# A hybrid decoder trunk on one core: the low part of the attention result made on GpSimd, and forget-gate steps with one operand in PSUM

## The chip, the cores and the metric

The kernel runs on one NeuronCore of a Trainium2 chip. A core has five engines with instruction queues of their own: TensorE (PE in the profile; its weight loads are shown as PEld), VectorE (DVE), ScalarE (ACT), GpSimd (POOL) and SyncE (SP, which here issues most DMAs). Each engine runs its queue in order; between engines, semaphores keep the order. SBUF is the working memory, and PSUM the memory into which TensorE writes. The metric is the device time of one execution in microseconds.

## The reference

Two layers over 512 tokens of width 1024 in float32. The first has a short gated convolution and a pooling mixer, the second (the odd layer) a forgetting attention and a Conformer convolution; each is followed by an output projection, a layer norm, a SwiGLU with 2816 hidden channels, and a layer norm. The part that the change touches is the attention of the odd layer:

```
log_f = log_sigmoid(p[..., gate columns] + forget_b)          # 8 heads
cum   = cumsum(log_f, axis=1)
logits[t, s] = q_t . k_s / 8 + cum[t] - cum[s],  causal
y_c   = softmax(logits) @ v                                   # 8 heads of 64
y     = concat([y_c, y_d]) @ w_out                            # y_d: the Conformer branch
```

## The kernel before

**Numbers.** Every float32 operand of a large product is split in two: a high part, which ACT writes as a copy rounded to the format fp32r, and a low part, the source minus the high part. A product is three matmuls (`mm3`, lines 88 to 90: high by high, low by high, high by low). The helper `split` makes both parts; its line 84 is the copy on ACT and its line 85 the subtraction, on DVE unless another engine is passed. In the profile, line 85 is therefore most of the subtractions in the program, told apart by the tile that they write.

**Order of the work.** A scheduler orders the instructions of the engines from a simulated timeline, with priorities; in the attention the order on TensorE is that of the code (a manual schedule), and the other engines are still ordered by the scheduler. `wk`, `wtp` and `rawp` are pools of SBUF buffers (2, 8 and 3 buffers to a tag), so an instruction that writes a new tile waits until the tile that held the buffer has been read.

**The odd layer**, in the order of its stages:

- *Conformer input and convolution* (`conv`, lines 448 to 469). Four blocks of 128 channels and 31 taps. Two and a large part of a third run on DVE, one multiply-add of 128x512 to a tap with the running sum in PSUM (L466, tile `cv`, with `convs` for the last); ACT starts such a block at L454. The rest are products on ACT (L459, `prod`) that GpSimd adds up (L460, `convs`). L469 on DVE joins a DVE and a GpSimd part. These run in the background of all that follows.
- *Forget gates* (`forget_gates`): some twenty small steps on 128x32 values, mostly on DVE, in the SBUF tile `gates`: z, -|z|, its exponential e, r = 1/(2+e), s1 = e*r, s2 = s1*s1, a polynomial in s2 (L510, seven steps) and lf, split into `lfh` and `lfl`.
- *Sums* (`cumulate`): eight matmuls (L575) against a triangle into the PSUM bank `py`; the rows and their negatives, each in two parts, go to the tile `aug` (L578 and L580 on ACT, L579 and L581 on DVE). `add_cum` (L634) copies rows of it by DMA into the operand tiles `qk` of a head.
- *Projections*: queries and keys of a head (`qk_proj`, weights `wqh` and `wql`, the latter made by GpSimd for four heads' worth at a time), values (`value_proj`, matmuls of 128x256 in the bank `fl`). `operands` (L623 to L629) splits a head's query and key and thereby frees its `fl` bank; L624 and L627 are its DVE steps.
- *Attention*, a loop over heads h = 0 to 7. The table `SEQ` sets the order in each round: S0, S1, S2 are scores and softmax of head h (L651 to L662; L658 and L661 on DVE, L660 and L662 on ACT), T0 and T1 the transposes of the probabilities of head h-1 with their split into `th` (ACT) and `tl` (DVE), W the product with the values of head h-1 (`weigh`, L692 on TensorE), and F0 to F3 a part of the projection of head h+2 or, in the last two rounds, of the output projection. With the statistics of the convolution (`conv_stats`, L711 to L717, in rounds 4 and 5) goes a power on GpSimd (L166, `rs`); `conv_swish` (L731 to L740, in round 6) ends that branch.
- *`weigh`* adds the two halves of a head's result in `yatt` (L696, L697); after the second head of a pair it splits the pair into `yc`, the left operand of the output projection. There are four pairs, j = 0 to 3.
- *The late affine* (`late_affine`, L202) multiplies and adds the norm's parameters to the residual stream, 16 instructions on GpSimd in this layer.
- *Output projection*: its weights `w` are loaded by `load_split` with the low part on GpSimd (L85, 128x1024).

Of the kernel before, what the change touches and what calls it, by code (L numbers as in the profile page):

```python
# [14 lines left out]
ALU = mybir.AluOpType  # L15
# [11 lines left out]
NH = 8  # L27
# [31 lines left out]
def trunk(ctx, tc, x, ev_w_in, ev_conv_w, ev_pool_w, ev_pool_scale, ev_w_out, od_w_in,  # L59
# [13 lines left out]
    def psum(tag=None):  # L73
        tag = tag or next(turn)
        return banks.tile([P, 512], F32, tag=tag, name=tag, bufs=BANKS[tag])

    def tpsum():
        return psum("tp")
# [3 lines left out]
    def split(hi, lo, src, eng=None):  # L82

        nc.scalar.activation(hi, src, AF.Copy)  # L84
        (eng or nc.vector).tensor_tensor(lo, src, f32(hi), op=ALU.subtract)  # L85
# [344 lines left out]
    def odd_mixer():  # L430
# [3 lines left out]
        V = nc.vector  # L434
        G = nc.gpsimd
        with tc.tile_pool(name="odd", bufs=1) as op:
# [6 lines left out]
            yc = [op.tile([P, 2, 2, S], F32R, tag="yc", name="yc", bufs=2) for _ in range(2)]  # L443
# [31 lines left out]
            def forget_gates():  # L475

                fraw = rawp.tile([P, KD, P], F32, tag="raw", name="fraw")[:, :, :NH]
                nc.sync.dma_start(fraw, w_in[:, FC:FC + NH].rearrange("(k p) c -> p k c", p=P))
                fw = op.tile([P, KD, 2 * NH], F32R, tag="fw", name="fw")
                split(fw[:, :, 0:NH], fw[:, :, NH:], fraw)  # L480
                fb = small32[:, 32:64].rearrange("p (t h) -> p t h", h=NH)
                nc.sync.dma_start(fb, bass.AP(tensor=od_forget_b.tensor, offset=od_forget_b.offset,
                                              ap=[[0, P], [0, NT], [1, NH]]))
                pf = psum("py")
                for k in range(KD - 1):
                    nc.tensor.matmul(pf[:2 * NH, :], fw[:, k, :], xh[:, k, :], start=k == 0, stop=False)
                for k in range(KD):
                    nc.tensor.matmul(pf[:NH, :], fw[:, k, :NH], xl[:, k, :], start=False, stop=False)
                nc.tensor.matmul(pf[:2 * NH, :], fw[:, KD - 1, :], xh[:, KD - 1, :], start=False, stop=True)
                fT = wk.tile([2 * NH, S], F32, tag="sg", name="fT")  # L490
                nc.scalar.activation(fT, pf[:2 * NH, :], AF.Copy)
                tp = tpsum()
                for t in range(NT):
                    nc.tensor.transpose(tp[:, t * 16:(t + 1) * 16], fT[:, t * P:(t + 1) * P], ident[:16, :16])
                tpv = tp[:, :64].rearrange("p (t c) -> p t c", c=16)
                small = wk.tile([P, S], F32, tag="h", name="gates")
                z, nz, e, r, s1, s2, w, lf = (small[:, i * 32:(i + 1) * 32].rearrange("p (t h) -> p t h", h=NH)
                                              for i in range(8))
                V.tensor_tensor(z, tpv[:, :, 0:NH], fb, op=ALU.add)
                V.tensor_tensor(z, tpv[:, :, NH:], z, op=ALU.add)  # L500
                V.scalar_tensor_tensor(nz, z, -1.0, z, op0=ALU.mult, op1=ALU.min)
                nc.scalar.activation(e, nz, AF.Exp)

                V.tensor_scalar(r, e, 2.0, None, op0=ALU.add)
                V.reciprocal(r, r)
                V.tensor_tensor(s1, e, r, op=ALU.mult)
                V.tensor_tensor(s2, s1, s1, op=ALU.mult)
                V.tensor_scalar(w, s2, 1.0 / 17.0, None, op0=ALU.mult)
                for c in (15, 13, 11, 9, 7, 5, 3):
                    V.scalar_tensor_tensor(w, w, 1.0 / c, s2, op0=ALU.add, op1=ALU.mult)  # L510
                V.scalar_tensor_tensor(w, w, 1.0, s1, op0=ALU.add, op1=ALU.mult)
                V.tensor_scalar(z, z, 0.0, None, op0=ALU.min)
                V.scalar_tensor_tensor(lf, w, -2.0, z, op0=ALU.mult, op1=ALU.add)
                split(lfh, lfl, lf)

            for j in range(4):
                if j == 0:
                    ws = [load_cols(w_in, DC + i * DH + n * P, eng=G if n >= DG else None)
                          for n in range(DFIRST) for i in range(2)]
                    accs = [psum(tag) for _, tag in zip(ws, ("sc", "sc", "py", "fl"))]  # L520
                    project(accs, ws, SPLIT)
                elif j >= DFIRST:
                    ws = [load_cols(w_in, DC + i * DH + j * P, eng=G) for i in range(2)]
                    accs = [psum("fl" if j % 2 else "sc") for _ in range(2)]
                    project(accs, ws, ALL)
                pv, pg = accs[2 * j:2 * j + 2] if j < DFIRST else accs
                sg = wk.tile([P, S], F32, tag="sg", name="sg")
                nc.scalar.activation(sg, pg, AF.Sigmoid)
                hp = op.tile([P, S + KCONV - 1], F32, tag="hp", name="hp", bufs=4)
                nc.gpsimd.memset(hp[:, 0:KCONV - 1], 0.0)  # L530
                V.tensor_tensor(hp[:, KCONV - 1:], pv, sg, op=ALU.mult)
                with tc.high_priority(offset=-CP):
                    conv(hp, j)
                if j == FPOS:
                    forget_gates()
# [146 lines left out]
            y32 = {}  # L682

            def weigh(h, th, tl):
                j, i = h // 2, h % 2
                if i == 0:
                    y32[j] = wk.tile([P, S], F32, tag="h", name="yatt")
                py = psum("py")
                terms = [(p, kb) for kb in range(NT) for p in (th, tl)]
                terms.append(terms.pop(1))  # L690
                for m, (p, kb) in enumerate(terms):
                    nc.tensor.matmul(py[:, kb * P:], vs[kb][:, h, :, :].rearrange("p a c -> p (a c)"),  # L692
                                     p[:, OFF[kb]:OFF[kb] + S - kb * P],
                                     start=m == 0, stop=m == len(terms) - 1)
                tmp = wk.tile([HD, S], F32, tag="sg", name="tmp")
                nc.scalar.activation(tmp, py[up, :], AF.Copy)  # L696
                V.tensor_tensor(y32[j][i * HD:(i + 1) * HD, :], py[lo, :], tmp, op=ALU.add)  # L697
                if i == 1:
                    split(yc[j // 2][:, j % 2, 0, :], yc[j // 2][:, j % 2, 1, :], y32[j])

            yds = []

# [95 lines left out]
            for h in range(NH):  # L798
                probs, stages = softmax(h, T[h])
                for i, op_ in enumerate(seq):  # L800
                    g = h if i > seq.index("W") else h - 1
                    if op_[0] == "S":
                        stages[int(op_[1])]()
                    elif op_[0] == "F":
                        fill[h][int(op_[1])]()
                    elif g >= 0 and op_ == "W":
                        weigh(g, *pt[g][:2])
                    elif g >= 0 and op_[0] == "T":
                        if g not in pt:
                            pt[g] = transpose_p(last if g < h else probs)  # L810
                        pt[g][2 + int(op_[1])]()
                    run((h, i))
                last = probs
# [4 lines left out]
            for t, op_ in zip(B, (tail + [None, None])[:2]):  # L818
                proj.first(0, (t,))
                if op_:  # L820
                    pt[NH - 1][2 + int(op_[1])]()
            weigh(NH - 1, *pt[NH - 1][:2])
            for i in range(1, 3):
                proj.first(i, [t for t in range(NT) if t not in done[i]])
# [33 lines left out]
```

## Time and profile before

| | |
|---|---|
| median of 3 runs | 1119.0 us (1117.41 to 1124.48) |
| profiled execution, its own time | 1118.16 us |
| span in its profile, first to last instruction | 1116.4 us |
| mean granted clock of TensorE | 0.991 |
| attention of the odd layer, with its convolution | about 535 to 715 us of the span |

The page of the profile gives busy time by engine, then the span in 40 slices (a digit is a tenth of the slice; PEclk is the clock granted to TensorE), then the chain of work that ended last, and groups of instructions by line. Rows of single instructions show start, length, engine, line, operation, output and inputs (partitions x elements, type), and, in brackets, how long the engine had stood idle before it and for whom it waited.

### The profile page before, as it was taken

To read this page: it belongs to the slowest core of one execution; us is meant where nothing else is said; L and a number is where in the kernel's file an instruction comes from. 1 tells how busy PE (TensorE), PEld (TensorE's weight loads), DVE (VectorE), ACT (ScalarE), POOL (GpSimd) and SP (SyncE) were. 2 spreads that over 40 slices of the span, in tenths; PEclk is the share of its full clock that TensorE was granted. 3 is DMA by queue.
4 is the path that set the end of the run, shared out by engine and by line. 5 is a ranking of instruction groups with operands and counts; after the bars stand their busy time and mean duration, and the time that the engine had idled before them with its cause. 6 is when DMAs were issued, how large, how long until landed. Compare 5 with 4: busy or idle time off the path is not lost.

```text
span 1116.4 us, 13508 instructions
## 1 busy us (share of the span) xinstructions
PE 1079.8 (97%) x5371; PEld 910.6 (82%) x5371; DVE 547.4 (49%) x821; ACT 395.5 (35%) x613; POOL 176.1 (16%) x160
## 2 busy tenths in 40 slices
PE   7999999999999999999999958999999999999997
PEld 7888898888888888889878746889888888888886
DVE  4845364633333322436689978564553333332426
ACT  4333134222233221223566838634232222222210
POOL 2000300000000000012797942520000000000003
PEclk9999999999999999999999979999999999999999
DMA  6423403343333222440332221333343333332312
GB/s 202 125 88 116 144 1 114 114 116 101 102 97 94 95 95 95 135 130 2 87 104 75 88 85 58 95 95 95 95 132 95 95 95 100 104 98 95 109 42 76
DMA packets 150332, 108.30 MB, mean 97 GB/s; under 512 B 5256, under 2 KB 131768, under 8 KB 150270
## 3 DMA queue, kind: packets, MB, share of 16 engines
q1 hardware_dynamic: 149648, 107.11, 31.9%
q8 instruction: 42, 0.69, 0.2%
q10 hardware_dynamic: 622, 0.34, 0.1%
q14 instruction: 20, 0.16, 0.1%
HBM read 103.17 MB, written 2.10 MB: 94 GB/s over the span
## 4 chain that ended last, share of the span: by engine, by line
PE 85%; DVE 7%; ACT 3%; POOL 3%; issue 1%; DMA 1%; SPq 0%; POOLq 0%; ACTq 0%
PE fl L88 11%; PE fl L89 11%; PE fl L90 11%; PE sc L89 9%; PE sc L90 9%; PE sc L88 9%; PE py L88 4%; PE py L89 4%; PE py L90 4%; PE cv L89 4%; PE cv L90 4%; PE cv L88 4%; DVE cv L466 2%; POOL convs L460 1%; DVE yc L85 1%
## 5 line engine op out<-in xcount | busy, mean ns | idle before, releaser
L84 ACT ACTIVATE w<-raw 128x1024 fp32r<-128x1024 f32 x176 | 185.9, 1060 | 538.1 <-PE sc L89 180.7
L85 DVE TENSOR_TENSOR w<-raw,w 128x1024 fp32r<-128x1024 f32 x148 | 180.7, 1224 | 287.5 <-ACT w L84 287.5
L85 POOL TENSOR_TENSOR w<-raw,w 128x1024 fp32r<-128x1024 f32 x28 | 67.4, 2415 | 450.6 <-ACT w L84 427.5
L89 PE MATMUL sc<-xl,w 128*128 128x512 f32 (+1 forms) x360 | 129.9, 361 | 0.0
L90 PE MATMUL sc<-xh,w 128*128 128x512 f32 (+1 forms) x360 | 129.6, 361 | 0.0
L88 PE MATMUL sc<-xh,w 128*128 128x512 f32 (+1 forms) x360 | 129.4, 362 | 0.0
L88 PE MATMUL fl<-xh,w 128*128 128x512 f32 (+1 forms) x352 | 128.6, 366 | 0.0
L89 PE MATMUL fl<-xl,w 128*128 128x512 f32 (+1 forms) x352 | 128.4, 365 | 0.0
L90 PE MATMUL fl<-xh,w 128*128 128x512 f32 (+1 forms) x352 | 128.3, 365 | 0.0
L166 POOL TENSOR_TENSOR rs<-rs,neghalf 128x1 f32<-128x1 f32 x20 | 14.4, 722 | 417.9 <-DVE rs L165 417.9
L89 PEld LDWEIGHTS sc<-xl,w 128*128 128x128 f32 x360 | 68.0, 189 | 10.3
L90 PEld LDWEIGHTS sc<-xh,w 128*128 128x128 f32 x360 | 68.0, 189 | 10.2
L88 PEld LDWEIGHTS sc<-xh,w 128*128 128x128 f32 x360 | 67.6, 189 | 10.4
L89 PEld LDWEIGHTS fl<-xl,w 128*128 128x128 f32 x352 | 66.5, 189 | 10.6
L88 PEld LDWEIGHTS fl<-xh,w 128*128 128x128 f32 x352 | 66.4, 189 | 10.6
L90 PEld LDWEIGHTS fl<-xh,w 128*128 128x128 f32 x352 | 66.3, 189 | 10.6
L89 PE MATMUL fl<-w,hh 128*128 128x512 f32 (+1 forms) x176 | 66.3, 377 | 0.0
L88 PE MATMUL fl<-w,hh 128*128 128x512 f32 (+1 forms) x176 | 66.1, 376 | 0.0
L90 PE MATMUL fl<-w,hl 128*128 128x512 f32 (+1 forms) x176 | 66.1, 376 | 0.0
L466 DVE SCALAR_TENSOR_TENSOR cv<-hp,par,cv 128x512 f32<-128x512 f32 x84 | 62.9, 749 | 5.2 <-ACT cv L454 3.9
L89 PE MATMUL py<-xl,w 128*128 128x512 f32 (+1 forms) x160 | 58.9, 368 | 0.0
L88 PE MATMUL py<-xh,w 128*128 128x512 f32 (+1 forms) x160 | 58.9, 368 | 0.0
(360 smaller groups left out, 2066.9 us busy)
## 6 DMA issues: line engine op xcount, KB each, us to landing
raw<-in_ffn_w_in SPq DMA_DIRECT2D x88, 512.0 KB
raw<-in_ffn_w_out SPq DMA_DIRECT2D x44, 512.0 KB
raw<-in_od_w_in SPq DMA_DIRECT2D x20, 512.0 KB
raw<-in_ev_w_in SPq DMA_DIRECT2D x16, 512.0 KB
raw<-in_ev_w_out SPq DMA_DIRECT2D x8, 512.0 KB
raw<-in_od_w_out SPq DMA_DIRECT2D x8, 512.0 KB
x<-in_x SPq DMA_DIRECT2D x4, 512.0 KB
qk<-qk SPq DMA_DIRECT2D x16, 128.0 KB
```

The source lines that it names most:

```text
L84: nc.scalar.activation(hi, src, AF.Copy)
L85: (eng or nc.vector).tensor_tensor(lo, src, f32(hi), op=ALU.subtract)
L88: nc.tensor.matmul(acc, lh, rh, start=start, stop=False)
L89: nc.tensor.matmul(acc, lh, rl, start=False, stop=False)
L90: nc.tensor.matmul(acc, ll, rh, start=False, stop=stop)
L166: nc.gpsimd.tensor_tensor(rs[:, 1:2], rs[:, 0:1], neghalf, op=ALU.pow)
L460: G.tensor_tensor(acc, acc, prod[:, i % 2, :], op=ALU.add)
L466: V.scalar_tensor_tensor(acc if i == KCONV - 1 else part, hp[:, i:i + S], tap(i), part, op0=ALU.mult, op1=ALU.add)
```

## The change

`weigh` passes GpSimd to `split` for the first three head pairs, so that the low part of `yc` is made there and not on DVE; the last pair stays on DVE. The high part stays on ACT.

In `forget_gates`, most of the values move from the SBUF tile to a PSUM bank (tag `py`), and where a step reads two of them, one is read from PSUM and the other from SBUF. For that, three values (z, s1 and s2) are made twice, once in each memory: three more DVE steps, written as `zp`/`zs`, `s1p`/`s1` and `s2p`/`s2`.

```
-                small = wk.tile([P, S], F32, tag="h", name="gates")
-                z, nz, e, r, s1, s2, w, lf = (small[:, i * 32:(i + 1) * 32].rearrange("p (t h) -> p t h", h=NH)
-                                              for i in range(8))
+                view = lambda tile, i: tile[:, i * 32:(i + 1) * 32].rearrange("p (t h) -> p t h", h=NH)
+                bank = psum("py")
+                small = wk.tile([P, S], F32, tag="h", name="gates")
+                zp, nz, e, r, s1p, s2p, w, lf = (view(bank, i) for i in range(8))
+                z, zs, r_, s1, s2, zmin = (view(small, i) for i in range(6))
                 V.tensor_tensor(z, tpv[:, :, 0:NH], fb, op=ALU.add)
-                V.tensor_tensor(z, tpv[:, :, NH:], z, op=ALU.add)
-                V.scalar_tensor_tensor(nz, z, -1.0, z, op0=ALU.mult, op1=ALU.min)
+                V.tensor_tensor(zp, tpv[:, :, NH:], z, op=ALU.add)
+                V.tensor_tensor(zs, tpv[:, :, NH:], z, op=ALU.add)
+                V.scalar_tensor_tensor(nz, zp, -1.0, zs, op0=ALU.mult, op1=ALU.min)
                 nc.scalar.activation(e, nz, AF.Exp)
                 V.tensor_scalar(r, e, 2.0, None, op0=ALU.add)
-                V.reciprocal(r, r)
-                V.tensor_tensor(s1, e, r, op=ALU.mult)
-                V.tensor_tensor(s2, s1, s1, op=ALU.mult)
-                V.tensor_scalar(w, s2, 1.0 / 17.0, None, op0=ALU.mult)
+                V.reciprocal(r_, r)
+                V.tensor_tensor(s1p, e, r_, op=ALU.mult)
+                V.tensor_tensor(s1, e, r_, op=ALU.mult)
+                V.tensor_tensor(s2p, s1p, s1, op=ALU.mult)
+                V.tensor_tensor(s2, s1p, s1, op=ALU.mult)
+                V.tensor_scalar(w, s2p, 1.0 / 17.0, None, op0=ALU.mult)
                 for c in (15, 13, 11, 9, 7, 5, 3):
                     V.scalar_tensor_tensor(w, w, 1.0 / c, s2, op0=ALU.add, op1=ALU.mult)
                 V.scalar_tensor_tensor(w, w, 1.0, s1, op0=ALU.add, op1=ALU.mult)
-                V.tensor_scalar(z, z, 0.0, None, op0=ALU.min)
-                V.scalar_tensor_tensor(lf, w, -2.0, z, op0=ALU.mult, op1=ALU.add)
+                V.tensor_scalar(zmin, zp, 0.0, None, op0=ALU.min)
+                V.scalar_tensor_tensor(lf, w, -2.0, zmin, op0=ALU.mult, op1=ALU.add)
                 split(lfh, lfl, lf)
...
-                    split(yc[j // 2][:, j % 2, 0, :], yc[j // 2][:, j % 2, 1, :], y32[j])
+                    split(yc[j // 2][:, j % 2, 0, :], yc[j // 2][:, j % 2, 1, :], y32[j], G if j < 3 else V)
```

Since the scheduler orders the engines anew, instructions that the diff does not name change places on DVE, ACT, GpSimd and SP, and the eight matmuls of the sums on TensorE. The prediction shows where. In the changed kernel the lines behind the gates are numbered 5 higher (L579 is L584 there).

GpSimd's queue from the last convolution sums to the statistics, as the change moves it, with rows in the form line, operation, output and inputs, shape, count; `x_76` and `x_77` are tiles of the residual stream:

```order
-L202 TENSOR_TENSOR x_76<-x_76,gb 128x512
-L85 TENSOR_TENSOR wql<-raw,wqh 128x8x64
+L202 TENSOR_TENSOR x_76<-x_76,gb 128x512 x2
+L85 TENSOR_TENSOR wql<-raw,wqh 128x8x64 x2
 L202 TENSOR_TENSOR x_77<-x_77,gb 128x512 x2
-L460 TENSOR_TENSOR convs<-convs,prod 128x512
 L85 TENSOR_TENSOR wql<-raw,wqh 128x8x64 x2
-L85 TENSOR_TENSOR w<-raw,w 128x1024
-L460 TENSOR_TENSOR convs<-convs,prod 128x512
-L85 TENSOR_TENSOR w<-raw,w 128x1024
+L85 TENSOR_TENSOR yc<-yatt,yc 128x512
+L85 TENSOR_TENSOR w<-raw,w 128x1024 x2
```

Both convolution sums have left this place (they stand earlier in the queue), the weights of heads 6 and 7 come in pairs, and the subtraction for the first head pair stands behind the last of them.

DVE between the low part of the gates and head 0's softmax, before:

```order
L85 TENSOR_TENSOR lfl<-gates,lfh 128x32
L466 SCALAR_TENSOR_TENSOR cv<-hp,par,cv 128x512
L85 TENSOR_TENSOR v<-fl,v 128x4x64
L466 SCALAR_TENSOR_TENSOR cv<-hp,par,cv 128x512 x4
L579 TENSOR_TENSOR aug<-py,aug 8x512
```

and in the changed kernel:

```order
L85 TENSOR_TENSOR lfl<-py,lfh 128x32
L466 SCALAR_TENSOR_TENSOR cv<-hp,par,cv 128x512
L85 TENSOR_TENSOR v<-fl,v 128x4x64
L466 SCALAR_TENSOR_TENSOR cv<-hp,par,cv 128x512
L85 TENSOR_TENSOR v<-fl,v 128x4x64
L466 SCALAR_TENSOR_TENSOR cv<-hp,par,cv 128x512 x2
L466 SCALAR_TENSOR_TENSOR convs<-hp,par,cv 128x512
L584 TENSOR_TENSOR aug<-py,aug 8x512
```

Between the gates' low part and the first row of sums stand the same number of convolution steps, but the last of them now ends a block.

## The prediction

> **What bounds the kernel now.** I read the page first: TensorE is busy almost everywhere, so only a stage in which it is not can give time back.
>
> ```profile
> PE 1079.8 (97%) x5371; PEld 910.6 (82%) x5371; DVE 547.4 (49%) x821; ACT 395.5 (35%) x613; POOL 176.1 (16%) x160
> PE   7999999999999999999999958999999999999997
> DVE  4845364633333322436689978564553333332426
> POOL 2000300000000000012797942520000000000003
> PEclk9999999999999999999999979999999999999999
> ```
>
> The digit 5 of PE and the 7 of PEclk stand in slice 24 (642 to 670 us), in the attention of the odd layer, where DVE and POOL are also at their fullest. So next come busy times per engine in short windows there (length; then PE, PEld, DVE, ACT, POOL; clock), and the list of who waited for whom.
>
> ```profile
> 577.00:587.00 10.00, 7.17 (x57) 6.82 (x56) 9.87 (x14) 4.39 (x8) 9.87 (x8) 1.00 0.45 112
> 635.00:643.00 8.00, 7.41 (x41) 5.71 (x39) 7.91 (x9) 5.30 (x12) 8.00 (x7) 1.00 0.16 36
> 643.00:654.00 11.00, 0.28 (x2) 0.00 (x0) 10.94 (x8) 1.39 (x3) 7.34 (x6) 0.66 0.27 95
> 654.00:660.50 6.50, 6.46 (x21) 5.09 (x22) 4.06 (x12) 3.84 (x11) 0.00 (x0) 0.52 0.00 0
> ...
> PE py L692 <- DVE tl L85: 11.2, 2, 10.8
> ACT pr L662 <- DVE sm L661: 14.9, 7, 10.6
> ```
>
> For 11 us TensorE does nothing, and it then runs 6.5 us at a granted clock of 0.52. The instructions in order of time show why (start, length, engine, line):
>
> ```profile
> 638.13 1.30 POOL L202 TENSOR_TENSOR x<-x,gb 128x512 f32<-128x512 f32 x1
> 638.85 12.04 DVE L85 TENSOR_TENSOR yc<-yatt,yc 128x512 fp32r<-128x512 f32 x1
> 639.36 1.31 POOL L85 TENSOR_TENSOR wql<-raw,wqh 128x512 fp32r<-128x512 f32 x1
> 640.60 2.57 POOL L202 TENSOR_TENSOR x<-x,gb 128x512 f32<-128x512 f32 x2
> 643.08 1.30 POOL L460 TENSOR_TENSOR convs<-convs,prod 128x512 f32<-128x512 f32 x1
> 644.30 2.52 POOL L85 TENSOR_TENSOR wql<-raw,wqh 128x512 fp32r<-128x512 f32 x2
> 646.74 2.38 POOL L85 TENSOR_TENSOR w<-raw,w 128x1024 fp32r<-128x1024 f32 x1
> 649.04 1.30 POOL L460 TENSOR_TENSOR convs<-convs,prod 128x512 f32<-128x512 f32 x1
> 650.88 0.73 DVE L466 SCALAR_TENSOR_TENSOR cv<-hp,par,cv 128x512 f32<-128x512 f32 x1
> 654.04 0.69 PE L692 MATMUL py<-tl,v 128*128 128x384 f32 x1 [10.77 <-DVE tl L85]
> ...
> L85 DVE TENSOR_TENSOR yc<-yatt,yc x4: 678/801/12035, 638.9 to 713.8; 128x512 fp32r<-128x512 f32 x4
> ```
>
> One subtraction on DVE, the low part of the first head pair, takes 12.04 us where the shortest of its kind takes 0.68. It ends at 650.89, just after GpSimd's unbroken row of two-operand instructions ends (649.04 + 1.30 = 650.34). Both its inputs lie in SBUF; DVE's neighbours that read an operand from PSUM (L466, 0.73) are not stretched. So I read it as DVE waiting for a read path that GpSimd doesn't let go while its queue is full. DVE runs in order: behind it stand L661, the tl splits that TensorE needs (10.77) and ACT's softmax (10.6).
>
> The page "SBUF — State Buffer" of the Trainium skill (Who interferes with whom) says that a DVE instruction with two SBUF inputs and a GpSimd one that reads SBUF exclude each other, and that the later one blocks until the first finishes. The trace agrees on who meets, not on how long: by that rule this subtraction would have got in at 639.43 and little would be there to gain; eight more GpSimd instructions went first.
>
> The gates, in the same dense stretch, show it small (shortest/median/longest ns): 183 with an operand in PSUM, up to 1339 without.
>
> ```profile
> L499 DVE TENSOR_TENSOR gates<-tp,small x1: 183/183/183, 573.6 to 573.6; 128x32 f32<-128x32 f32 x1
> L512 DVE TENSOR_SCALAR gates<-gates x1: 1154/1154/1154, 577.6 to 577.6; 128x32 f32<-128x32 f32 x1
> L504 DVE TENSOR_SCALAR gates<-gates x1: 1339/1339/1339, 578.6 to 578.6; 128x32 f32<-128x32 f32 x1
> L506 DVE TENSOR_TENSOR gates<-gates x1: 1219/1219/1219, 581.4 to 581.4; 128x32 f32<-128x32 f32 x1
> ...
> 586.51 0.36 PE L88 MATMUL fl<-w,xh 128*128 128x256 f32 x1 [2.83 <-DVE qk L627]
> ```
>
> **The change, term by term**, against the profiled execution: 1118.16 us (span 1116.4 and 1.76 around it); the median of the three is 1119.0, 0.8 above.
>
> *1. The stall at 638.85 goes: -10.8.* GpSimd takes the subtraction, in another place of its queue:
>
> ```order
> -L460 TENSOR_TENSOR convs<-convs,prod 128x512
>  L85 TENSOR_TENSOR wql<-raw,wqh 128x8x64 x2
> -L85 TENSOR_TENSOR w<-raw,w 128x1024
> -L460 TENSOR_TENSOR convs<-convs,prod 128x512
> -L85 TENSOR_TENSOR w<-raw,w 128x1024
> +L85 TENSOR_TENSOR yc<-yatt,yc 128x512
> +L85 TENSOR_TENSOR w<-raw,w 128x1024 x2
>  L166 TENSOR_TENSOR rs<-rs,neghalf 128x1 x2
>  L85 TENSOR_TENSOR w<-raw,w 128x1024
> +L85 TENSOR_TENSOR yc<-yatt,yc 128x512
>  L166 TENSOR_TENSOR rs<-rs,neghalf 128x1 x2
> ```
>
> It stands behind the last wql and is needed only by the output projection. It costs GpSimd what a wql costs:
>
> ```profile
> L85 POOL TENSOR_TENSOR wql<-raw,wqh 128x512 fp32r<-128x512 f32 x16 | 20.5, 1300 | 5.5 <-ACT wqh L84 5.5
> ```
>
> So 3 x 1.3 = 3.9 us on an engine that then waits (0.00 busy from 654 to 660.5 above). The two convolution sums that stood last now run before the late affine, so the normalization's statistics needn't wait for them. With the DVE instruction gone, five DVE steps of 0.15 to 0.7 lie between 638.85 and tl, which is then ready near 642; TensorE began its wait at 643.27 (654.04 - 10.77), so the whole of it goes. Bounds: 8, if head 4 then waits for GpSimd's queue, dry at 650.3, and 10.8.
>
> *2. The slow clock goes: -2.5.* In 6.5 us at clock 0.52 TensorE loses at most 6.46 x 0.48 = 3.1; I take 2.5, since some of it would be waits for the softmax. Bounds 0 and 3.1.
>
> *3. The gates: +1.0.* DVE loses its stretched steps (0.97 + 1.16 + 1.04 = 3.2 over 0.18 each in the three rows above, beside smaller ones) and gets three more steps of 0.18. That takes away TensorE's 2.83 at 583.7. But DVE's order changes too. Before, from the low part of the gates to the rows of sums (aug) and on to head 0's softmax:
>
> ```order
> L85 TENSOR_TENSOR lfl<-gates,lfh 128x32
> L466 SCALAR_TENSOR_TENSOR cv<-hp,par,cv 128x512
> L85 TENSOR_TENSOR v<-fl,v 128x4x64
> L466 SCALAR_TENSOR_TENSOR cv<-hp,par,cv 128x512 x4
> L579 TENSOR_TENSOR aug<-py,aug 8x512
> L85 TENSOR_TENSOR v<-fl,v 128x4x64
> L466 SCALAR_TENSOR_TENSOR cv<-hp,par,cv 128x512
> L581 SCALAR_TENSOR_TENSOR aug<-py,aug 8x512
> ```
>
> and in the changed kernel (L579 is L584 there, L581 is L586):
>
> ```order
> L85 TENSOR_TENSOR v<-fl,v 128x4x64
> L466 SCALAR_TENSOR_TENSOR cv<-hp,par,cv 128x512 x2
> L466 SCALAR_TENSOR_TENSOR convs<-hp,par,cv 128x512
> L584 TENSOR_TENSOR aug<-py,aug 8x512
> L466 SCALAR_TENSOR_TENSOR cv<-hp,par,cv 128x512 x2
> L586 SCALAR_TENSOR_TENSOR aug<-py,aug 8x512
> L466 SCALAR_TENSOR_TENSOR cv<-hp,par,cv 128x512 x2
> ```
>
> A convolution block now ends ahead of L584, and the two cv steps behind it open the next block. In all five convolution steps come ahead of the first softmax that came behind it, 5 x 0.73 = 3.7 us at most, and on TensorE the eight matmuls of the sums stand 34 value matmuls later.
>
> ```profile
> 596.78 0.28 PE L89 MATMUL fl<-w,xh 128*128 128x256 f32 x1
> 596.89 0.56 PE L575 MATMUL py<-tri,lfh 128*8 128x512 f32 x2
> 600.86 0.68 DVE L579 TENSOR_TENSOR aug<-py,aug 8x512 fp32r<-8x512 f32 x1
> 602.69 0.68 DVE L581 SCALAR_TENSOR_TENSOR aug<-py,aug 8x512 fp32r<-8x512 f32 x1
> 605.03 0.50 PE L653 MATMUL sc<-qk 68*128 68x512 f32 x1
> ```
>
> From 586.51 to 596.78 stand 86 value matmuls, 0.12 each. Without the wait the row starts at 583.7; 120 of them now precede the sums: 583.7 + 14.4 = 598.1, not 596.9. From the sums' start to head 0's scores (L653) the copies, L579, L581 and their DMAs took 8.1 us; kept, the scores start at 606.2, 1.2 later than 605.03, and TensorE, which has only 24 value matmuls left behind the sums (598.1 + 8 x 0.28 + 24 x 0.12 = 603.2), waits 3 us there. I take +1.0. Bounds: -2.8, if the chain of copies shortens as much, and +3. The five steps moved forward leave DVE less behind 635, which is in term 1.
>
> *4. Given back in head 4: +1.1.* When everything comes some 12 us earlier, the second out-projection weight does not: its DMA waits until GpSimd's third of the last wqls frees the buffer, before at about 645.6 (644.30 + half of 2.52), and takes 3.6 us (711.16 to 714.76 below, issue to the ACT copy that waits for it): 649. ACT has that copy in line ahead of head 4's softmax and would come to it near 648, when head 5's projection is out (some 4 us of TensorE after 643.3): 1.0 there. A further 0.1 is for DVE's L717 (L722), which frees the bank for the next statistics and now stands behind six instructions more. Before:
>
> ```order
> L715 BN_AGGR mv<-cst 128x2
> L165 TENSOR_SCALAR rs<-mv 128x1
> L717 TENSOR_SCALAR npair<-cv,mv,rs 128x512
> L85 TENSOR_TENSOR tl<-tp,th 128x512
> L658 TENSOR_REDUCE nm<-sc 128x1
> ```
>
> and now:
>
> ```order
> L720 BN_AGGR mv<-cst 128x2
> L165 TENSOR_SCALAR rs<-mv 128x1
> L632 TENSOR_TENSOR qk_4341<-fl,qk_4341 64x512
> L663 TENSOR_REDUCE nm<-sc 128x1
> L85 TENSOR_TENSOR tl<-tp,th 128x512
> L85 TENSOR_TENSOR tl<-tp,th 128x384
> L666 RECIPROCAL sm<-sm 128x1
> L663 TENSOR_REDUCE nm<-sc 128x1 x2
> L722 TENSOR_SCALAR npair<-cv,mv,rs 128x512
> ```
>
> Before, L717 waited 2.11 for GpSimd's rs, so most of that move is covered.
>
> ```profile
> 666.43 0.81 DVE L717 TENSOR_SCALAR npair<-cv,mv,rs 128x512 f32<-128x512 f32 x1 [2.11 <-POOL rs L166]
> ...
> 711.16 0.37 SPq L95 DMA_DIRECT2D raw<-in_od_w_out  x1
> 714.76 1.06 ACT L84 ACTIVATE w<-raw 128x1024 fp32r<-128x1024 f32 x1 [0.99 <-DMA raw<-in_od_w_out]
> ```
>
> Bounds 0 and 2.5. The second and third yc leave DVE at 0.7 each and meet an idle GpSimd; nothing taken. The first layer and both FFNs keep their instructions and their order.
>
> **Sum:** 1118.16 - 10.8 - 2.5 + 1.0 + 1.1 = 1107.0.
>
> **The rivals.**
> - *The gates pay too.* If the copies of the sums shorten as DVE does, term 3 is -2.8: 1103. For it: DVE was the chain's longest link there. Against: head 0's scores hang on a DMA behind the sums, and these come later.
> - *GpSimd becomes the bound.* Its row from 619 to 650 holds the same work plus 1.3; if head 4 needs its end, term 1 is 8 and term 2 about 1.5, with both givebacks: 1111. Against: the convolution sums now stand early, and head 6's wqls stand seven instructions ahead of its last weight split.
> - *It doesn't help.* If the 12 us were not the meeting of the two engines but a wait for that data, GpSimd's copy would take 12 us too and hold rs behind it: about 1118. The Trainium skill leans this way for another reason: "Perfetto Trace Analysis" (Optimizing Scalar/DVE Operations) warns that moving work between these two engines may not help, as they share a read port; no run here shows it yet.
> - *Slower.* The stall finds another victim: the convolution branch's last two-input instructions on DVE (yconv and its low parts, to 701.8), against GpSimd's row of weight splits.
>
> ```profile
> 701.08 0.69 DVE L85 TENSOR_TENSOR qk<-yconv,qk 128x512 fp32r<-128x512 f32 x1 [0.34 <-ACT qk L84]
> ...
> 708.73 2.40 POOL L85 TENSOR_TENSOR w<-raw,w 128x1024 fp32r<-128x1024 f32 x1 [20.95 <-PE tp L676]
> 711.76 9.94 POOL L85 TENSOR_TENSOR w<-raw,w 128x1024 fp32r<-128x1024 f32 x4 [0.63 <-ACT w L84]
> ```
>
> They are 7 us apart, since these splits wait for TensorE; if the earlier attention let them start 7 us sooner relative to it, DVE would stand 2.4 + 9.94 us and TensorE lose the clock again: 1107 + 12.3 + 2.5 = 1122.
>
> **How the numbers follow.** Forecast 1107 with its spread: 0.52; gates pay: 0.18; GpSimd the bound: 0.20; no help: 0.05; slower: 0.05. The best bounds give 1118.2 - 10.8 - 3.1 - 2.8 = 1101.5, the worst 1118.2 - 8 + 3 + 2.5 = 1115.7: range 1101 to 1115. A measurement of this kernel tells about 1% from no change, 11.2 us, so 1107.8 is the border, and my forecast lies on it. Faster: the 0.18 and 0.32 of the 0.52; same: the rest of it, 0.20 and 0.05; slower 0.05.
>
> **What would show it.** No DVE instruction above 2 us between 570 and 720; gate steps all near 0.2; PEclk without its 7; yc on POOL three times at 1.3; a wait of some 3 us of TensorE ahead of head 0's scores (L653, in the changed kernel L658), and short ones in head 4. I am wrong if a long DVE row is still there, or if TensorE waits for POOL in heads 3 to 5.

## The result and the profile after

The changed kernel takes **1101.43 us** (median of 4 runs, 1100.73 to 1102.10) where the kernel before takes 1118.70 in the same comparison: a ratio of 0.9845, 95% interval 0.9826 to 0.9865. It is 17.3 us faster; 11 to 12 were forecast, with 1101 as the lower end of the range. The profiled execution took 1100.73 us, its span 1099.0.

The page of the changed kernel: busy time by engine, then the forty slices of POOL and of the granted clock.

```profile
PE 1077.5 (98%) x5371; PEld 909.8 (83%) x5371; DVE 529.7 (48%) x821; ACT 395.4 (36%) x613; POOL 179.9 (16%) x163
...
POOL 2000300000000000012499972700000000000003
PEclk9999999999999999999999999999999999999999
```

PEclk has lost its 7, DVE is busy 17.7 us less (547.4 before) though it gave away only three subtractions, and POOL is busy 3.8 us more, the three subtractions of 1.3 each. Now who TensorE waited for between 560 and 730 us (total, times, longest):

```profile
PE sc L658 <- DMA qk<-aug: 3.1, 1, 3.1
PE tp L681 <- ACT pr L667: 1.5, 4, 0.6
...
PE cv L716 <- DVE sm L666: 0.5, 1, 0.5
PE fl L88 <- DVE qk L632: 0.5, 1, 0.5
```

The waits of 10.8 for DVE's tl and of 2.8 for qk are gone, and one of 3.1 has come, ahead of head 0's scores. Busy times by stage, in the windows used for the kernel before (length; PE, PEld, DVE, ACT, POOL; clock):

```profile
577.00:587.00 10.00, 10.00 (x84) 9.81 (x82) 9.87 (x25) 5.15 (x10) 9.65 (x8) 1.00 0.54 142
...
605.00:620.00 15.00, 15.00 (x72) 11.92 (x73) 14.01 (x30) 12.73 (x31) 12.36 (x11) 0.89 0.51 151
...
643.00:654.00 11.00, 10.46 (x62) 8.49 (x62) 7.90 (x20) 8.90 (x22) 7.83 (x6) 1.00 0.68 212
654.00:660.50 6.50, 6.50 (x43) 5.42 (x41) 5.41 (x14) 4.79 (x10) 3.40 (x3) 1.00 0.12 30
660.50:700.00 39.50, 37.03 (x203) 29.97 (x203) 26.41 (x59) 32.33 (x71) 13.39 (x9) 1.00 0.21 63
```

From 643 to 654 TensorE is busy for 10.46 us instead of 0.28, and the clock behind it is 1.00 instead of 0.52. The slow stretch has not vanished, it has shrunk and moved: 0.89 between 605 and 620, behind the new wait, where the kernel before had 1.00. The last window has a row of before that the prediction did not look at:

```profile
660.50:700.00 39.50, 34.49 (x196) 26.97 (x195) 31.45 (x73) 31.51 (x71) 9.33 (x7) 1.00 0.25 74
```

There TensorE idled for 5 us of 39.5, against 2.5 in the changed kernel (where the same window holds later work). Where the lead builds up can be read from the starts of the same matmul in the two traces:

| matmul | before | after | lead |
|---|---|---|---|
| head 0's first score that needs the sums (L653, now L658) | 605.03 | 604.94 | 0.1 |
| last transposes ahead of the stall (L676, L681) | 638.11 | 637.66 | 0.5 |
| first matmul of the weighted sum that needs `tl`, behind the stall (L692, L697) | 654.04 | 642.65 | 11.4 |
| first transposes for the statistics (L711, L716) | 660.10 | 645.84 | 14.3 |
| last transposes for the statistics | 680.78 | 663.57 | 17.2 |

Some 0.3 of each lead is there from the start of the program, ahead of all that the change touches (583.22 against 582.94 at head 0's first matmul).

What changed places, in order of time, on GpSimd and (second fence) on DVE:

```profile
641.80 2.56 POOL L85 TENSOR_TENSOR wql<-raw,wqh 128x512 fp32r<-128x512 f32 x2
644.28 1.33 POOL L85 TENSOR_TENSOR yc<-yatt,yc 128x512 fp32r<-128x512 f32 x1
645.53 4.78 POOL L85 TENSOR_TENSOR w<-raw,w 128x1024 fp32r<-128x1024 f32 x2
```

```profile
578.93 0.18 DVE L509 TENSOR_TENSOR py<-py,gates 128x32 f32<-128x32 f32 x1
...
581.29 0.19 DVE L511 TENSOR_TENSOR py<-py,gates 128x32 f32<-128x32 f32 x1
```

The subtraction costs GpSimd 1.33 where DVE stood 12.04, and no gate step takes more than 0.35.

### The profile page after: what moved, and what is told of

Its sections match the earlier page's. It is cut to its first block, busy times and chain, and to the rows that moved or that the text cites. A ratio compares the mean times of both kernels' runs of the same rounds, so it can differ in the third digit from the quotient of the medians.

```text
span 1099.0 us, 13519 instructions
## 1 busy us (share of the span) xinstructions
PE 1077.5 (98%) x5371; PEld 909.8 (83%) x5371; DVE 529.7 (48%) x821; ACT 395.4 (36%) x613; POOL 179.9 (16%) x163
## 4 chain that ended last, share of the span: by engine, by line
PE 93%; DVE 2%; ACT 2%; DMA 1%; POOL 1%; issue 1%; SPq 0%; POOLq 0%
PE fl L88 12%; PE fl L90 12%; PE fl L89 12%; PE sc L88 9%; PE sc L90 9%; PE sc L89 9%; PE py L88 4%; PE py L89 4%; PE py L90 4%; PE cv L89 4%; PE cv L90 4%; PE cv L88 4%; PE tp L132 1%; DMA x<-in_x 1%; DVE cv L466 1%
```

## The experiments

Ratios are to the kernel before, run beside it on the same chip, with 95% intervals. The code cuts are shortened.

### The two halves apart

*The low parts alone* (the gates as before):

```diff
-                    split(yc[...], yc[...], y32[j])
+                    split(yc[...], yc[...], y32[j], G if j < 3 else V)
```

> Half of the change alone: the low parts of head pairs 0 to 2 go to GpSimd, the gates stay as before. Theory A (the whole gain is the one 12 us subtraction and what hung on it; the gates are worth nothing): about 1102 us, that is 11 of the stall, 3 of the slow clock and 3 of later waits gone; TensorE still waits 2.8 at 583.7 for the gates and not 3.1 ahead of head 0's scores. Rival B (both halves are needed): above 1106.

Measured: 1109.65 us, ratio 0.9923 (0.9906 to 0.9939): 8.6 faster, half of what theory A expected; rival B's "above 1106" is what came. GpSimd's last convolution sum, and TensorE's transposes that need it:

```profile
652.11 1.28 POOL L460 TENSOR_TENSOR convs<-convs,prod 128x512 f32<-128x512 f32 x1
```

```profile
648.00 0.27 PE L711 MATMUL cv<-ident,convs 128*128 128x128 f32 x1
653.45 0.90 PE L711 MATMUL cv<-ident,convs 128*128 128x128 f32 x3 [5.18 <-POOL convs L460]
```

The stall for DVE is gone, and 5 us later TensorE stands still again, now for GpSimd: the sum is still the second last of its row, now behind a subtraction more. Behind the wait the matmuls start 0.43 apart instead of 0.23, which cost another 2.7 us. Where the changed kernel is ahead of this one can again be read from the same matmul in the two traces: by 1.4 at head 0's first matmul (584.39 against 582.94, a difference that is there from the start of the program), by 2.6 at head 0's scores (607.55 against 604.94), by 2.2 at the first statistics and by 9.5 at the second (662.54 against 653.02). So 1.2 comes between the gates and the scores (the clock was 0.91 from 587 to 605 here, behind the wait of 2.8 for the gates), and 7.4 at the convolution sum.

*The gates alone* (all low parts on DVE): the other part of the diff.

> The other half alone: the gates in PSUM, all low parts of the attention on DVE as before. Theory A: 1118 within 2 us, with the subtraction of head pair 0 again at 8 to 12 us and ended by the end of GpSimd's row. Rival B (the gates' new order of the queues is what helped): 1108 or less, and no DVE instruction above 2 us after 620.

Measured: 1110.37 us, ratio 0.9932 (0.9918 to 0.9947): 7.9 faster, where theory A expected nothing and rival B more: neither number. The subtraction of head pair 0 on DVE, and the last instruction of GpSimd's row:

```profile
638.55 9.05 DVE L85 TENSOR_TENSOR yc<-yatt,yc 128x512 fp32r<-128x512 f32 x1
```

```profile
644.68 2.37 POOL L85 TENSOR_TENSOR w<-raw,w 128x1024 fp32r<-128x1024 f32 x1
```

It still waits for the end of the row (644.68 + 2.37 = 647.05), but the row is 3.3 us shorter: the two convolution sums have left its end. TensorE's longest wait there is 5.3 us instead of 10.8. So both halves act on GpSimd's row; their gains alone add to 16.5, together they are 17.3.

### Is it the order of GpSimd's queue, or the gates?

*The late affine issued later*, with the low parts on GpSimd and the gates as before:

```diff
-XG = (3, 8)
+XG = (4, 3)
```

> Low parts on GpSimd, gates as before, and the late affine issued later (from head 3's stage 8 to head 4's stage 3): in GpSimd's queue the last convolution sums and the subtraction now stand ahead of it, TensorE's order is that of before. Theory O (what the gates' half of the change brought is the other order of GpSimd's queue): the wait of 5.2 for the convolution sums and 2.7 of slow clock behind it go, 1102 us within 1.5. Rival (the gates in PSUM are needed for themselves): 1107 or more.

Measured: 1112.01 us, ratio 0.9936 (0.9911 to 0.9962): by the time, the rival's number, but from a cause that neither names. The convolution sums were early, as meant, and TensorE was 15.3 us ahead of the kernel before at its first statistics (644.84 against 660.10). At the second ones 6.2 were left (661.24 against 667.39). GpSimd's queue, and who waited:

```profile
638.81 17.42 POOL L202 TENSOR_TENSOR x<-x,gb 128x512 f32<-128x512 f32 x14 [1.36 <-DMA gb<-in_ln_ffn_g]
...
659.68 0.57 POOL L166 TENSOR_TENSOR rs<-rs,neghalf 128x1 f32<-128x1 f32 x1
```

```profile
PE cv L711 <- DVE npair L717: 9.8, 1, 9.8
```

The reciprocal root of the statistics (rs) stood behind the row that had been moved out of the way. The question stayed open; with the low parts alone it was a convolution sum at the end of GpSimd's row that TensorE waited for, here it is this root.

*Two taps of the last convolution block back on DVE*, so that no convolution sum stands at the row's end:

```diff
-GT = (0, 31, 0, 4)
+GT = (0, 31, 0, 2)
```

> Low parts on GpSimd, gates as before, and two of the four taps that the last convolution block gave to ACT and GpSimd go back to DVE (GT from (0, 31, 0, 4) to (0, 31, 0, 2)): no convolution sum stands behind the late affine's row any more, nothing else in GpSimd's row is later. Theory O (the gates' half brought its gain by taking the convolution sums off the end of GpSimd's row): the wait of 5.2 and its 2.7 of slow clock go, 1101 to 1103 us, with the wait of 2.8 for the gates still there. Rival (the gates in PSUM are needed for themselves): 1107 or more.

Measured: 1107.26 us, ratio 0.9901 (0.9886 to 0.9916): by the time, the rival's number (1107 or more). Who TensorE waited for:

```profile
PE fl L88 <- DVE qk L627: 3.4, 3, 2.1
...
PE cv L711 <- DVE convs L469: 1.5, 1, 1.5
```

But the wait of 5.2 for GpSimd is gone without the gates in PSUM, which is what the theory says; the time was lost earlier, ahead of head 0's scores, where DVE had the two taps more. A gate step (L501) now took 2.20, and head 0's score started at 609.07 instead of 605.03. From there to the last transposes for the statistics it gained 14.5 us on the kernel before (609.07 against 605.03, then 670.29 against 680.78); by the same two matmuls the low parts alone gained 10.2 and the whole change 17.1. So the place of the convolution sums accounts for a large part of what the gates' half brings; that it accounts for all of it is not shown.

### What the meeting is

*One operand in PSUM.* The subtraction stays on DVE, in the kernel before:

```diff
+ nc.scalar.activation(hip, f32(hi), AF.Copy)        # hip: a PSUM bank, head pair 0 only
- V.tensor_tensor(lo, y32[j], f32(hi), op=ALU.subtract)
+ V.tensor_tensor(lo, y32[j], hip, op=ALU.subtract)
```

> The kernel before, with one edit: for head pair 0, ACT copies the high part once more, into a PSUM bank, and DVE's subtraction reads it there; the same engine, the same place in its queue, the same data, one operand in PSUM. Theory A (DVE waits for a read path that GpSimd holds while both its operands lie in SBUF): the subtraction takes 0.7, the stall of 10.8 goes, 1102 to 1105 us. Rival (it waits for its data, or a full GpSimd queue slows DVE whatever it reads): it still takes about 12, 1118 us.

Measured: 1108.68 us, ratio 0.9916 (0.9901 to 0.9930). DVE's row, and TensorE's transposes:

```profile
639.57 0.68 DVE L704 TENSOR_TENSOR yc<-yatt,tp 128x512 fp32r<-128x512 f32 x1
```

```profile
640.31 0.47 PE L676 MATMUL tp<-ident,pr 128*128 128x128 f32 x1 [4.62 <-DVE yc L704]
```

0.68 instead of 12.04, in the middle of the same GpSimd row, and without even a wait for the instruction that was running there. That speaks for the meeting over SBUF operands; the wait for data is ruled out by the kernel with the reordered loop (below), whose subtraction takes 1.80 with the same data at the same place. One reservation comes from the count found below: the subtraction met 14 instructions since GpSimd's last pause here, one fewer than in the kernel before, so by this run alone it could have got in with both operands in SBUF too. The changed kernel has the missing case: behind 17 instructions of an unbroken row, two splits `tl` with one operand in PSUM took 1.15 together (at 640.12), as they do when GpSimd rests (1.14 at 652.84 in the kernel before). The gain is smaller than expected: the transposes waited 4.6 us for the bank that was taken from them, and head 0's scores came 2.4 later (607.43 against 605.03), at a clock of 0.85 from 587 to 605.

*The meeting by itself.* GpSimd runs a row of two-operand instructions, and VectorE is started into it. A boundary is the moment between two instructions of the row.

> The meeting by itself; leaves out the whole computation. In each stage GpSimd runs an unbroken row of 14 instructions of 128x512 (or 7 of 128x1024) with two operands in SBUF, and early in it DVE is started on instructions of one kind. Theory A1 (DVE gets in only when GpSimd leaves a gap): 128x512 with two SBUF operands takes 10 us or more in every row, and so do the small ones. Theory A2 (DVE gets in at each boundary of GpSimd's instructions, and the 12 us is a rare case): none above 1.9 (2.9 in the row of 128x1024). Theory A3 (size decides): 128x512 takes over 10 us, 128x32 under 1.5. With an operand in PSUM 0.7 throughout; with no row 0.7 for 512, 0.2 for 32.

Measured: in 15 stages each instruction with two SBUF operands got in at GpSimd's next boundary, except one. Two stages with the same row (`mixed`), DVE's rows:

```profile
91.08 1.44 DVE L109 TENSOR_TENSOR dd<-da,db 128x512 f32<-128x512 f32 x1
...
108.98 14.86 DVE L112 TENSOR_TENSOR dr<-da,db 128x512 fp32r<-128x512 f32 x1
```

The second waited through eleven boundaries until the row was dry. So both things exist, and none of A1, A2, A3 holds (A2, with 12 us as a rare case, is nearest). One operand in SBUF is no way out: the 128x512 step with a single operand there (L118) took 1.17 and 1.37 beside the row and 0.43 without it. The output type differed, so that was tried next.

> The meeting by itself once more; leaves out the whole computation. In the first such run one instruction of VectorE out of all took 14.86 us, until GpSimd's row was dry; it was the only one whose output was float32r (all others wrote float32 and got in at the next boundary, 1.4 us). Here float32r and float32 outputs are set against each other in the same rows, with and without a semaphore to wait for, small ones too. Theory F (the output type decides): each float32r output of 128x512 takes 10 us or more in the row that mixes kinds, each float32 one under 2. Theory W (it was the missing wait on a semaphore): the float32r one that waits for ScalarE takes under 2, and the float32 one into a place nobody reads takes over 10. Theory P (phase, chance): no order in it.

```profile
69.96 14.85 DVE L122 TENSOR_TENSOR do<-da,db 128x512 f32<-128x512 f32 x1
...
88.17 1.04 DVE L113 TENSOR_TENSOR dr<-da,db 128x128 fp32r<-128x128 f32 x1
...
105.65 14.35 DVE L113 TENSOR_TENSOR dr<-da,db 128x32 fp32r<-128x32 f32 x1
...
123.36 0.68 DVE L125 TENSOR_TENSOR dr<-pa,db 128x512 fp32r<-128x512 f32 x1
```

Float32 lost too (14.85), 128x32 lost (14.35) where 128x128 got in (1.04): neither type nor size decides; an operand in PSUM passes (0.68). Theory W's two numbers came: 1.11 for the instruction that waited for ScalarE (at 52.41), 14.85 for the one into a place nobody reads. But the 128x128 one got in without such a wait, and the sixteen meetings below have one and the same instruction both ways. The same test inside the kernel, with a float32 output in place of float32r:

```diff
- V.tensor_tensor(lo, y32[j], f32(hi), op=ALU.subtract)
+ V.tensor_tensor(y32[j], y32[j], f32(hi), op=ALU.subtract)   # head pair 0
+ nc.scalar.activation(lo, y32[j], AF.Copy)
```

> The kernel before, with one edit: for head pair 0 DVE's subtraction writes float32 in place (over the attention result) instead of float32r, and ACT rounds that into the low part. Same engine, same place in the queue, both operands in SBUF. Theory F (output type decides whether it gets in at a boundary): 1.5 to 2 us instead of 12.0; the stall of 10.8 goes, but GpSimd's convolution sums still stand at its row's end, so about 1108 to 1110 as with the low parts on GpSimd alone. Rival (two SBUF operands are enough, whatever the output): 8 to 12 us again, 1117 to 1120.

Measured: 1118.13 us, ratio 1.0 (0.9986 to 1.0014); DVE's row:

```profile
638.62 12.05 DVE L702 TENSOR_TENSOR yatt<-yatt,yc 128x512 f32<-128x512 f32 x1
```

Theory F fell. Sixteen meetings of one and the same instruction followed, in two rows without gaps and one with:

> The meeting by itself, the same VectorE instruction (128x512, float32, two operands in SBUF) sixteen times; leaves out the whole computation. Six times in the row that mixes kinds without gaps, four times in the row of strided instructions without gaps, six times in a row of which each fifth instruction needs the one before it. Theory P (without a gap it is a race that is lost for good when it is lost once): in the mixed row some take 1.4 and some about 14.8, nothing between; in the row with gaps each takes 1.4, or about 5 where the first boundaries are lost, never more. Rival (it depends on the kind of row): all six in the mixed row alike.

```profile
12.64 1.44 DVE L126 TENSOR_TENSOR do<-da,db 128x512 f32<-128x512 f32 x1
30.54 14.85 DVE L126 TENSOR_TENSOR do<-da,db 128x512 f32<-128x512 f32 x1
48.74 1.44 DVE L126 TENSOR_TENSOR do<-da,db 128x512 f32<-128x512 f32 x1
...
193.28 1.44 DVE L126 TENSOR_TENSOR do<-da,db 128x512 f32<-128x512 f32 x1
```

In the ten stages without gaps it got in and lost by turns, in both kinds of row; in the six with a gap after each fifth instruction it always got in at 1.44. The turns are not chance: after a lost stage GpSimd had to wait for VectorE before its next row, after a won one it ran on without a pause. So the length of the unbroken row was varied:

> The meeting by itself, the same VectorE instruction (128x512, float32, two operands in SBUF) fourteen times; leaves out the whole computation. In the runs so far it got in at GpSimd's next boundary each time when GpSimd's row had a pause no longer than 6.3 us (6 instructions) before, and waited until the row was dry each time when the row had run unbroken for 18 us or more (15 instructions or more). Here each row begins with a pause and VectorE comes after 3, 5, 7, 9, 11, 13, 15 and 17 instructions of 1.25 us, after 9, 17 and 25 short ones (128x256), and after 4, 6 and 8 long ones (128x1024). Theory T (the unbroken time decides): the long row of 8 (some 19 us) loses though it has few instructions, and 17 short ones (some 11 us) get in if 9 of 1.25 us do. Theory N (the number of instructions decides): 17 short ones lose if 17 of 1.25 us lose, and 8 long ones get in. Rival (neither: the pause is not it): all fourteen get in, or they alternate.

DVE's rows for 11 and 13 instructions of 1.25 us, 9 and 17 short ones, and 8 long ones:

```profile
98.21 1.44 DVE L126 TENSOR_TENSOR do<-da,db 128x512 f32<-128x512 f32 x1
125.33 9.98 DVE L126 TENSOR_TENSOR do<-da,db 128x512 f32<-128x512 f32 x1
...
204.28 0.90 DVE L126 TENSOR_TENSOR do<-da,db 128x512 f32<-128x512 f32 x1
225.50 8.38 DVE L126 TENSOR_TENSOR do<-da,db 128x512 f32<-128x512 f32 x1
...
324.56 2.52 DVE L126 TENSOR_TENSOR do<-da,db 128x512 f32<-128x512 f32 x1
```

**The number of instructions decides.** Counting the two small ones that frame each row, VectorE got in after 5 to 13 instructions since the last pause and lost after 15 or more: 8.38 behind 19 short ones (12.3 us since the pause), 2.52 behind ten of which eight are long (19.1 us). Counted the same way, the three earlier runs by themselves fall in line: VectorE got in behind at most 6 and lost behind 20 or 21. In the kernel before, 15 instructions stood between GpSimd's last pause and the subtraction at 638.85, 15 again with the float32 output, 16 with the gates alone (9.05). And a gate step of the kernel before met 14, one of them a memset that reads nothing, and got in at the next boundary:

```profile
584.03 0.39 DVE L507 TENSOR_TENSOR gates<-gates 128x32 f32<-128x32 f32 x1
```

GpSimd's row had run for 19.4 us at that moment, and for 19.4 us at 638.85, so here too it is not the time.

*Gaps in the kernel's own row.* The kernel before, all on DVE, but the late affine multiplies and adds tile by tile, so that an addition needs the multiplication that is issued just before it:

```diff
-        with tc.high_priority(offset=-CP):
+        with tc.high_priority(offset=-CP), tc.manual_schedule(engines={mybir.EngineType.Pool}):
```

> The kernel before, its subtraction still on DVE with two operands in SBUF; in the late affine GpSimd now adds right behind each multiplication of the same tile, so that each second instruction of that row waits for the one before it and leaves a gap (0.08 in the row of dependent instructions measured by itself). Theory G (in a row without gaps DVE can lose every boundary; a gap lets it in): the subtraction takes 1.3 to 4 us instead of 12.0 and the wait of 10.8 is gone or under 3; 1106 to 1111 us, if no wait for GpSimd's queue takes its place. Rival (a full queue is enough, gaps or not): 8 to 12 us again, 1116 to 1120.

Measured: **1103.56 us**, ratio 0.9865 (0.9848 to 0.9883). DVE's subtraction, and the GpSimd instruction that it held up:

```profile
639.74 1.80 DVE L85 TENSOR_TENSOR yc<-yatt,yc 128x512 fp32r<-128x512 f32 x1
```

```profile
640.95 1.75 POOL L85 TENSOR_TENSOR wql<-raw,wqh 128x512 fp32r<-128x512 f32 x1
```

1.80 instead of 12.04, with no subtraction moved and no gate touched. The scheduler put other instructions between most of the pairs: only three stand back to back and leave a gap of 0.08 (at 635.97, 644.02 and 646.61). The first was enough, three instructions ahead of the subtraction. The order of one loop alone gains 14.1 us, where the change gains 17.3 and 1106 to 1111 were expected here. Not all of it is the gap: the scheduler set two convolution sums earlier as well, and what each is worth was not taken apart.

### A faster version

*The changed kernel with the gates' sums earlier*: the third and fourth value block and the sums are put in order by hand on TensorE.

```diff
-PRE = "C Q0 A0 Q1 V00 V01 A1 V10 V11"
+PRE = "Q0 Q1 V00 V01 ( V10 C V11 ) A0 A1"     # ( ): tc.manual_schedule(engines={PE})
```

> The changed kernel, with the eight matmuls of the gates' sums set between the third and the fourth value block (24 matmuls earlier on TensorE). If the gates are ready (lfl ended at 594.0) the sums start at 594.8 instead of 597.7, the wait of 3.1 ahead of head 0's scores goes to about 0.2, and the slow clock behind it (1.4) with it: 1097 to 1098.5 us. Rival: the row of sums on DVE and ACT meets other work there and the wait stays over 2: 1100 to 1102.

Measured: **1098.72 us** (1097.62 to 1099.66), ratio 0.9814 (0.9793 to 0.9835), against 0.9845 of the change. TensorE's sums and head 0's score, first in the changed kernel, then here:

```profile
597.67 0.56 PE L580 MATMUL py<-tri,lfh 128*8 128x512 f32 x2
...
604.94 0.50 PE L658 MATMUL sc<-qk 68*128 68x512 f32 x1 [3.08 <-DMA qk<-aug]
```

```profile
595.77 0.56 PE L580 MATMUL py<-tri,lfh 128*8 128x512 f32 x2
...
602.68 0.40 PE L658 MATMUL sc<-qk 68*128 68x512 f32 x1
```

The wait of 3.08 is gone, and the clock stays at 1.00 behind it. The time is 0.2 above the range of the theory; a wait of 1.0 for GpSimd's convolution sum has come at the statistics. The runs of the two kernels do not overlap (1100.73 is the fastest of the changed kernel), but the intervals of their ratios just do, so the gain of 2 to 3 us is likely rather than certain.

## Why the prediction was right, and where it was not

The time lies at the edge of the range, and that it lies inside is partly luck: the lower end took the gates at -2.8 and the giveback of head 4 at 0, and these measured some -0.2 and -2.9, two misses that cancel. The stall and the clock behind it are not luck.

- **Step 1, the stall, -10.8: right.** The lead grew from 0.5 to 11.4 across it: 10.9. Its reason held in part. The two engines do meet over SBUF operands (0.68 with one in PSUM), and DVE did wait until GpSimd's queue was dry; what the prediction could not say, why it passed eight boundaries here and none elsewhere, is the count of instructions since GpSimd's last pause. The page "SBUF — State Buffer" of the Trainium skill (Who interferes with whom) has the later engine wait until the first finishes: that agrees with the meetings up to 13 instructions (1.44), and differs from those from 15 on (14.85, and 12.04 in the kernel). (Two counts are off by one, without effect: four DVE steps, not five, stand ahead of tl, and L722 stands behind seven instructions more, not six.)
- **Step 2, the slow clock, -2.5: right**, 2.9 measured (11.4 to 14.3).
- **Step 3, the gates, +1.0: the path right, the price wrong.** The sums started at 597.67 (598.1 forecast) and the wait ahead of the scores was 3.08 (3 forecast). From the sums to the scores took 7.3 us instead of the 8.1 that were kept, so the scores came at 604.94, not 606.2. A slow stretch behind that wait was left out: 605 to 620 ran at 0.89, and the matmuls behind the scores lost 1.4 against those of before within 4 us. A wait of 1.2 for ACT, that the kernel before had just there, went. Together the term was some -0.2: the lead was 0.3 ahead of the gates' wait and 0.5 ahead of the stall.
- **What step 3 missed is larger.** Without the gates' half the low parts on GpSimd gain 8.6 instead of 17.3. As far as the runs show, most of what the gates' half adds comes from what the scheduler did with it: it took the convolution sums off the end of GpSimd's row. That is 7.4 us by the matmuls of the two traces; 1.2 more lies between the gates and head 0's scores. The prediction saw the move of the sums and gave it no price. Its rival "GpSimd becomes the bound" (1111) is near what happens without it: 1109.65.
- **Step 4, given back in head 4, +1.1: the step that failed.** It was a gain of 2.9 (14.3 to 17.2). The weight's DMA was late as forecast, and ACT waited 0.77 for it at 646.80, but TensorE did not wait for ACT. What was overlooked is what follows the stall: in the kernel before TensorE waited for DVE four more times until 681, 2.66 in all. In the changed kernel only the first of the four has a twin, of 0.54:

```profile
667.39 0.63 PE L711 MATMUL cv<-ident,convs 128*128 128x128 f32 x4 [0.59 <-DVE npair L717]
...
668.83 0.44 PE L692 MATMUL py<-tl,v 128*128 128x384 f32 x1 [0.40 <-DVE tl L85]
...
673.48 0.63 PE L711 MATMUL cv<-ident,convs 128*128 128x128 f32 x4 [1.04 <-DVE npair L717]
...
680.78 0.63 PE L711 MATMUL cv<-ident,convs 128*128 128x128 f32 x4 [0.63 <-DVE sm L661]
```

  That DVE and ACT came out of the stall with full queues, and that these waits are its wake, is a reading of these rows. The runs speak for it in part. From the first to the last transposes for the statistics the kernel before took 20.7, and 20.7 again with the float32 output, which stalled as long. The changed kernel took 17.7, and 17.4 with one operand in PSUM and with the gaps, which did not stall. But the gates alone, which stalled for 9.05, took 17.4 too, so not every such stall leaves a wake; why this one did stays open.

- **The rivals.** "It doesn't help" and the page "Perfetto Trace Analysis" of the Trainium skill (Optimizing Scalar/DVE Operations), which doubts that a move between these two engines helps since they share a read port: the low parts alone gained 8.6, since GpSimd runs them in its own queue (1.33 in the changed kernel) and nobody waits for their result soon. "Slower" did not come: the last low part still met the row of weight splits and got in at the next boundary (0.92). "The gates pay too" (1103) lay nearest to the time, for another reason than its own.

## What to carry to other kernels

In these runs a VectorE instruction with two SBUF operands lost one instruction of GpSimd's row at most (1.44, or 2.52 beside long ones) as long as that row had had a pause shortly before; behind 15 or more instructions without one it waited until that queue was dry, and everything behind it waited too. Before moving work to another engine, break the row: put dependent instructions next to each other, or let an operand come from PSUM. And when a stall goes, price what follows it too (further waits, slow clock), and look at what now stands last in the queue of the engine that was let off.

## What the runs showed that was not expected

- GpSimd's row locks VectorE out by count, not by time: ten instructions since the pause, 19.1 us, let it in; 19 instructions, 12.3 us, did not. With 14 there is the one gate step that got in; no run tells why the number is what it is.
- A pause of 0.08 us, left by an instruction that needs the one before it, is enough to start the count anew (six of six meetings in the row with gaps, and the kernel with the reordered loop).
- When VectorE gets in, GpSimd pays: its next instruction took 1.71 instead of 1.26.
- The slow clock does not follow each short wait. Behind the wait of 2.8 at 583.7 the kernel before kept 1.00; behind the same wait (2.7 to 2.8) the clock from 587 to 605 was 0.85 in the kernel whose subtraction reads PSUM, and 0.91 with the low parts alone and with the reordered loop. From head 0's first matmul to its scores these took 24.3, 23.2 and 23.0 us, where the kernel before took 21.8. The page "TensorE: Matmul & The Clock Gate" of the Trainium skill (What's actually happening) lowers the clock after at least one idle window of about 3.4 us. These waits are shorter, so the three slow runs do not fit that figure; what decides is open.
